# In a hybrid attention layer, the weighted sums of one pair of heads are put in front of the scores of the next

## The chip, the cores and the metric

The kernel runs on one core of a Trainium2 chip. The metric is the device time in microseconds (us) of one execution. The core has five engines with their own instruction queues: TensorE (PE, matrix products; its weight loads are shown as PEld), VectorE (DVE), ScalarE (ACT), GpSimd (POOL), and SyncE (SP), which here issues most of the DMAs. An engine works through its own queue in order and waits for the others by semaphores.

## What is computed

One decoder layer on 512 positions of width 1024, in float32, with two attention branches of 8 heads of 64 each, side by side:

```
h = rms_norm(x);  qa,ka,va,za, qb,kb,vb,zb, gl_a,gl_b = split(h @ w_in)
a: softmax(rms_norm(qa) @ rms_norm(ka).T * scale + T5 bias, causal) @ va
b: w[t,s] = sigmoid(z) * prod_{s<j<t} (1 - sigmoid(z[t,j])),  z = qb @ kb.T * scale;   w @ vb
y = sigmoid(gl_a + b_a) * ((oa * silu(za)) @ w_up_a) + sigmoid(gl_b + b_b) * ((ob * silu(zb)) @ w_up_b)
x + y @ w_out
```

Branch a is a block-sparse attention, but with 512 positions every block of the past is chosen, so the kernel computes plain causal attention.

## The kernel before

The projections come first: q, k and v of branch a and v of branch b for all positions. Everything that remains of the input projection (gates `za`, `zb`, `gl`, and q, k of branch b) is cut into chunks of 128 output columns (`chunk_ct`). One chunk is 24 matmuls of 512 columns: eight slices of the width, each in three products (L179 to L181) of a value that is split into a high and a low part (`hi`, `lo`; `wh` is written by ACT at L138, the remainder `wl` by DVE at L140, from a weight tile `wr` that SP loads at L129).

The main loop (L601) runs over eight pairs of heads, pairs 0 to 3 of branch a, 4 to 7 of branch b. In each pair:

- `scores` computes the products of q and k of both heads. The heads lie in the upper and the lower 64 partitions, and their matmuls alternate: 24 in all (L418), of 512, 384, 256 and 128 columns, each in three products of split values.
- `softmax` (ACT and DVE) or `stick` (two sigmoids on ACT, a scan and a product on DVE) makes the weights `p` of a head, `turn` transposes them on DVE in blocks (L461), `put` stores them to DRAM (SP, L468), and `get` brings them back fully transposed as `pt` (issued by ACT, L475).
- `fill` puts chunks of projections between these steps, by the list FILLS.
- `finish` of the pair before calls `weighted`: eight matmuls (L487) with `pt` of both heads, alternating, into the two halves of one bank `po`, head 0 into partitions 0 to 63 and head 1 into 64 to 127. These run in plain float32. DVE multiplies the result with the gate (`oa` or `ob`, L491), and `split_o` splits it into `oh` (ACT, L522) and `ol` (DVE, L523), which the `up` products use later.

The order in which instructions stand on an engine is set by a scheduler that takes the source's order as a priority and moves an instruction back when it reckons that its operands come late. Accumulation banks come from two pools, "pj" with two banks for chunks and `po`, "s" with six for scores.

Of the kernel before, what the change touches and what calls it, by code (L numbers as in the profile page):

```python
# [57 lines left out]
def hybrid_layer(ctx: ExitStack, tc: tile.TileContext, x, xT, w, rel, out):  # L58
# [15 lines left out]
    def bank(tag, name):  # L74
        return pp.tile([P, S], F32, tag=tag, bufs=BANKS[tag], name=name)
# [23 lines left out]
    def sum_w(names, done):  # L99

        with tc.issue_after(G.tensor_copy(turn_of, done[:1, :1].bitcast(F32)).ins):  # L101
            for n in range(2):
                for name in names:
                    if n == 0:
                        sums[name] = vp.tile([P, H // 2, 2, P], F32, tag="v", name=name).rearrange("p a b d -> p (a b d)")
                    blk = TERMS[name[:2]][n]
                    src = sums[blk + name[2]] if blk[0] == "T" else w[WO + BLOCKS.index(blk + name[2])]
                    nc.gpsimd.dma_start(sums[name], src, **({"accum_op": ALU.add} if n else {}))
# [165 lines left out]
    def load_bias(h):  # L274
        bt = oms[2 + h % 2][:, :S]
        nc.sync.dma_start(bt, bass.AP(tensor=e_dr.tensor, offset=e_dr.offset + h * TW, ap=[[1, P], [1, S]]))
        return bt
# [129 lines left out]
    def scores(br, p, q, k, res):  # L407

        (qh, ql), (kh, kl) = q[p], k[p]
        for grp in ((3,), (2,), (1, 0)):  # L410
            ps = [bank("s", f"s{br}{2 * p + b}{grp[0]}") for b in range(2)]
            c = 0
            for i in grp:
                n = (i + 1) * P
                for m, (x, y) in enumerate(((qh, kl), (ql, kh), (qh, kh))):
                    for b in range(2):
                        o = slice(b * HD, (b + 1) * HD)
                        T.matmul(ps[b][:, c:c + n], x[o, i * P:(i + 1) * P], y[o, :n], start=m == 0, stop=m == 2)  # L418
                for b in range(2):
                    res[2 * p + b][i] = ps[b][:, c:c + n]  # L420
                c += n
# [32 lines left out]
    def turn(br, h, rows):  # L454
        turned = tp.tile([P, 4, BLK[-1], 32], F32, tag="turned", bufs=2, name=f"turned{br}{h}")
        for i in (3, 2, 1, 0):
            for j in range(0, i + 1, 2):
                n = min(2, i + 1 - j)
                step = (BLK[j + 1] - 1 - BLK[j]) if n == 2 else 1
                at = BLK[j] + i - j  # L460
                V.transpose(turned[:, :, at:at + (n - 1) * step + 1:step, :].rearrange("p q j r -> p j q r"),  # L461
                            rows[i][:, j * P:(j + n) * P].rearrange("p (j q c) -> p j q c", j=n, q=4))
        return turned

    def put(br, h, turned):
        dr = dp.tile([P, 4 * PQ], F32, tag="pd", bufs=4, name=f"pd{br}{h}")
        for a in range(4):
            nc.sync.dma_start(bass.AP(tensor=dr.tensor, offset=dr.offset + a * PQ,  # L468
                                      ap=[[4 * PQ, 32], [32 * 4 * PQ, 4], [1, PQ]]),
                              turned[a * 32:(a + 1) * 32].rearrange("c q k r -> c q (k r)"))  # L470
        return dr

    def get(br, h, dr):
        pt = tp.tile([P, 4 * PQ], F32, tag="pt", bufs=4, name=f"pt{br}{h}")
        nc.scalar.dma_start(pt, dr)  # L475
        return pt
# [3 lines left out]
    def weighted(tag, br, p, vv, pts):  # L480

        po = bank(tag, f"po{br}{p}")
        for j in range(NT):
            for b in range(2):
                o, c = slice(b * HD, (b + 1) * HD), (2 * p + b) * HD
                src = pts[b].rearrange("p (a n) -> p a n", a=4)[:, :, BLK[j] * 32:BLK[j + 1] * 32]
                T.matmul(po[o, :].rearrange("p (a n) -> p a n", a=4)[:, :, j * 32:], vv[j][:, c:c + HD], src,  # L487
                         start=j == 0, stop=j == NT - 1, skip_group_check=True)
        ocol[br, p] = u = slot(f"o{br}{p}")
        dst, z = (by_block((mirror if br == "a" else blocks)(x)) for x in (u, zr[br, p]))  # L490
        V.tensor_tensor(dst, po.rearrange("p (a i r) -> p a i r", a=4, i=4).rearrange("p a i r -> p i a r"), z,  # L491
                        op=ALU.mult)
# [25 lines left out]
    def split_o(br, p):  # L518
        u = ocol[br, p]
        oH[br, p] = slot(f"oh{br}{p}", F32R)  # L520
        oL[br, p] = slot(f"ol{br}{p}", F32R)
        A.activation(oH[br, p], u, AF.Copy)  # L522
        V.tensor_tensor(oL[br, p], u, oH[br, p].bitcast(F32), op=ALU.subtract)  # L523
# [59 lines left out]
    def fill(tag="pj"):  # L583

        home[0] = tag
        for kind, i in fills.pop(0):
            make[kind](i)
# [4 lines left out]
    def head(m, b):  # L592
        return PAIRS[m][0], 2 * PAIRS[m][1] + b

    def finish(m, tag="s"):

        br, p = PAIRS[m]
        weighted(tag, br, p, v_of[br], [done.pop((m, b)) for b in range(2)])
        split_o(br, p)

    for m, (br, p) in enumerate(PAIRS):  # L601
        q, k = (qa, ka) if br == "a" else (qb, kb)
        sc, rw = {h: [None] * NT for h in (2 * p, 2 * p + 1)}, {h: [None] * NT for h in (2 * p, 2 * p + 1)}
        scores(br, p, q, k, sc)
        if m > 1:
            finish(m - 1, "pj")
        for b in range(2):
            h = 2 * p + b
            bias = load_bias(h) if br == "a" else None
            (softmax if br == "a" else stick)(h, sc[h], rw[h], bias, (3, 2, 1, 0))  # L610
            done[m, b] = put(br, h, turn(br, h, rw[h]))
            fill()
            if not b:
                done[m, 0] = get(*head(m, 0), done[m, 0])
        for b in range(2):
            if m == 1 and not b:
                finish(0)
            if not b:
                done[m, 1] = get(*head(m, 1), done[m, 1])
            if (m, b) in SUMS:  # L620
                sum_w(SUMS[m, b], done[m, b])
            fill("pj" if b or not fills[1] and m < len(PAIRS) - 1 else "s")
# [87 lines left out]
    for c in range(2):  # L710
        hi, lo = load_w()
        for t, ps, a, b in parts:
            for kk in range(2):
                k = 2 * c + kk
# [76 lines left out]
```

## Time and profile before

| | |
|---|---|
| time, median of three runs | 391.37 us (391.12 to 391.51) |
| the profiled execution's own time | 391.4 us |
| its span, from the first to the last instruction | 389.6 us |
| PE busy | 385.0 us, 99% |
| DVE, ACT, POOL busy | 68%, 50%, 13% |
| mean granted TensorE clock | 0.999 of full speed |

A share of busy time is an average over the whole program. What an edit costs is read from the place where it stands: from the list of who waited for whom, and from the timeline of the engine that others wait for.

### The profile page before, as it was taken

Reading aid. Unit: us, or ns where it says so; the run is one execution under the profiler, and the core shown is the slowest. Engines: PE = TensorE matmul, PEld = TensorE weight load, DVE = VectorE, ACT = ScalarE, POOL = GpSimd, SP = SyncE. Lnnn points to the kernel's source line nnn. Section 1 sums busy time; section 2 is a strip of 40 time slices with the busy share of each in tenths; the row PEclk is TensorE's granted clock in tenths of the full one; section 3 lists DMA queues with packets and bytes.
Section 4 is the critical chain, followed back from the end, with each engine's and each line's share of the span. In section 5 each row is a group of like instructions: output and inputs, shape, how many; then the busy total and the mean of one; then the engine's idle time right before and its main releaser. Section 6 shows DMA issues by size and latency. Waiting matters only on the chain.

```text
span 389.6 us, 5321 instructions
## 1 busy us (share of the span) xinstructions
PE 385.0 (99%) x1853; PEld 308.8 (79%) x1853; DVE 266.8 (68%) x535; ACT 194.6 (50%) x341; POOL 51.9 (13%) x100
## 2 busy tenths in 40 slices
PE   8999999999999999999999999999999999999996
PEld 5888888888887878878788878878878878888885
DVE  4824995854879477295596398489459534999962
ACT  5684522945778466264552472363254232359540
POOL 1018966000000000000000100100000000232110
PEclk9999999999999999999999999999999999999999
DMA  7977259982496946827526776776772842798935
GB/s 266 330 269 241 112 157 290 307 273 73 133 259 226 295 178 151 306 74 240 175 68 192 257 202 182 246 205 170 263 215 67 271 148 89 217 245 301 196 76 175
DMA packets 36091, 79.29 MB, mean 203 GB/s; under 512 B 3929, under 2 KB 16729, under 8 KB 36065
## 3 DMA queue, kind: packets, MB, share of 16 engines
q1 hardware_dynamic: 29584, 56.68, 45.0%
q0 software_dynamic: 2880, 9.44, 10.6%
q10 hardware_dynamic: 3600, 12.85, 9.9%
q8 instruction: 14, 0.23, 0.2%
q14 instruction: 13, 0.10, 0.1%
HBM read 62.15 MB, written 14.70 MB: 197 GB/s over the span
## 4 chain that ended last, share of the span: by engine, by line
PE 99%; DVE 0%; issue 0%
PE gl L179 8%; PE gl L181 7%; PE gl L180 7%; PE poa L487 2%; PE pob L487 2%; PE sb L418 2%; PE sa L418 2%; PE za L179 2%; PE kb L179 2%; PE zb L179 2%; PE za L180 2%; PE kb L181 2%; PE zb L181 2%; PE zb L180 2%; PE yb L181 2%; PE yb L180 2%
## 5 line engine op out<-in xcount | busy, mean ns | idle before, releaser
L140 DVE TENSOR_TENSOR wl<-wr,wh 128x1024 fp32r<-128x1024 f32 (+1 forms) x64 | 75.8, 1185 | 62.1 <-ACT wh L138 57.0
L138 ACT ACTIVATE wh<-wr 128x1024 fp32r<-128x1024 f32 (+1 forms) x64 | 65.8, 1028 | 41.4 <-DMA wr<-in_w 15.8
L179 PE MATMUL gl<-xl,wh 128*128 128x512 f32 x128 | 50.5, 395 | 0.0
L181 PE MATMUL gl<-xh,wh 128*128 128x512 f32 x128 | 49.9, 390 | 0.0
L180 PE MATMUL gl<-xh,wl 128*128 128x512 f32 x128 | 49.8, 389 | 0.0
L513 ACT ACTIVATE gl<-gl,x 128x512 f32<-128x512 f32 x16 | 11.0, 690 | 41.7 <-PE gl L181 41.6
L179 PEld LDWEIGHTS gl<-xl,wh 128*128 128x128 f32 x128 | 24.0, 188 | 5.8 <-issue 1.0
L101 POOL COPY turn_of<-ptb 1x1 f32<-1x1 f32 x3 | 1.3, 433 | 202.0 <-DMA ptb<-pdb 202.0
L181 PEld LDWEIGHTS gl<-xh,wh 128*128 128x128 f32 x128 | 24.0, 188 | 5.1
L180 PEld LDWEIGHTS gl<-xh,wl 128*128 128x128 f32 x128 | 24.0, 188 | 4.8
L446 DVE TENSOR_TENSOR_SCAN sx<-om,begin 128x512 f32<-128x512 f32 (+3 forms) x32 | 24.9, 805 | 0.2 <-ACT om L442 0.2
L430 ACT ACTIVATE pa<-pa,m 128x512 f32<-128x512 f32 (+3 forms) x32 | 17.8, 557 | 10.9 <-DVE m L428 9.0
L428 DVE CUSTOM_DVE_ANT_0 pa<-sa,om 128x512 f32<-128x512 f32 (+3 forms) x32 | 14.8, 477 | 10.9 <-PE sa L418 10.9
L461 DVE STREAM_TRANSPOSE turneda<-pa 128x256 f32<-128x256 f32 (+1 forms) x48 | 16.4, 376 | 0.1
L442 ACT ACTIVATE om<-sb 128x512 f32<-128x512 f32 (+3 forms) x32 | 14.6, 462 | 3.2 <-DVE sx L446 2.9
L461 DVE STREAM_TRANSPOSE turnedb<-pb 128x256 f32<-128x256 f32 (+1 forms) x48 | 15.9, 370 | 0.0
L444 ACT ACTIVATE pb<-sb 128x512 f32<-128x512 f32 (+3 forms) x32 | 14.7, 465 | 0.0
L448 DVE TENSOR_TENSOR pb<-pb,sx 128x512 f32<-128x512 f32 (+3 forms) x32 | 14.2, 471 | 0.0
L179 PE MATMUL za<-xl,wh 128*128 128x512 f32 x32 | 12.7, 396 | 0.0
L179 PE MATMUL kb<-xl,wh 128*128 128x512 f32 x32 | 12.6, 393 | 0.0
L179 PE MATMUL zb<-xl,wh 128*128 128x512 f32 x32 | 12.6, 393 | 0.0
L181 PE MATMUL zb<-xh,wh 128*128 128x512 f32 x32 | 12.5, 390 | 0.0
(305 smaller groups left out, 957.9 us busy)
## 6 DMA issues: line engine op xcount, KB each, us to landing
wr<-in_w SPq DMA_DIRECT2D x60, 512.0 KB, 5.4
pda<-turneda SPq DMA_DIRECT2D x32, 160.0 KB, 2.6
pta<-pda ACTq DMA_DIRECT2D x8, 640.0 KB, 6.0
pdb<-turnedb SPq DMA_DIRECT2D x32, 160.0 KB, 2.7
ptb<-pdb ACTq DMA_DIRECT2D x8, 640.0 KB, 4.5
xn<-in_x SPq DMA_DIRECT2D x8, 256.0 KB, 6.6
xs<-in_xT SPq DMA_DIRECT2D x8, 256.0 KB, 6.2
om<-e_dr SPq DMA_DIRECT2D x8, 256.0 KB, 6.5
```

Source lines behind the costliest of these rows:

```text
L138: A.activation(hi[:, a:b], raw[:, a:b], AF.Copy)
L140: low[c] = V.tensor_tensor(lo[:, a:b], raw[:, a:b], hi[:, a:b].bitcast(F32), op=ALU.subtract).ins
L179: T.matmul(ps, aH, bL, start=start, stop=False, skip_group_check=on)
L180: T.matmul(ps, aL, bH, start=False, stop=False, skip_group_check=on)
L181: T.matmul(ps, aH, bH, start=False, stop=stop, skip_group_check=on)
L418: T.matmul(ps[b][:, c:c + n], x[o, i * P:(i + 1) * P], y[o, :n], start=m == 0, stop=m == 2)
L428: V.tensor_tensor_reduce(p, sc[i], bias[:, S - n:], scale=1.0, scalar=3e38, op0=ALU.add, op1=ALU.min, accum_out=m[:, 0:1])
L430: A.activation(p, p, AF.Exp, bias=m[:, 0:1], scale=-1.0, accum_out=m[:, 1:2])
L444: A.activation(p, z, AF.Sigmoid)
L446: V.tensor_tensor_scan(sx[:, n - 1::-1] if n == S else sx[:, :n][:, ::-1], om[:, e - n:][:, ::-1], begin[:, S - n:][:, ::-1], 0.0, op0=ALU ...
L461: V.transpose(turned[:, :, at:at + (n - 1) * step + 1:step, :].rearrange("p q j r -> p j q r"), rows[i][:, j * P:(j + n) * P].rearrange("p ...
L487: T.matmul(po[o, :].rearrange("p (a n) -> p a n", a=4)[:, :, j * 32:], vv[j][:, c:c + HD], src, start=j == 0, stop=j == NT - 1, skip_group ...
```

## The change

The call of `finish` for the pair before stands in front of `scores` and not behind it, from pair 2 on.

```
     for m, (br, p) in enumerate(PAIRS):
         q, k = (qa, ka) if br == "a" else (qb, kb)
         sc, rw = ...
-        scores(br, p, q, k, sc)
         if m > 1:
             finish(m - 1, "pj")
+        scores(br, p, q, k, sc)
         for b in range(2):
...
```

The built programs show what the scheduler makes of it. First PE at the boundary of pair 2. In the program before, the last scores of pair 2 (`sa`), then the eight weighted matmuls of pair 1 (`poa`, from the transposed tiles `pta` of its two heads), then the next chunk (`gl`); the number behind a name counts tiles:

```order
L418 MATMUL sa_1446<-ka2h,qa2l 128x128
L418 MATMUL sa_1445<-ka2h,qa2h 128x128
L418 MATMUL sa_1446<-ka2h,qa2h 128x128
L487 MATMUL poa_1459<-pta_1274,vas_803 64x512
L487 MATMUL poa_1459<-pta_1361,vas_803 64x512
L487 MATMUL poa_1459<-pta_1274,vas_803 64x4x96
L487 MATMUL poa_1459<-pta_1361,vas_803 64x4x96
L487 MATMUL poa_1459<-pta_1274,vas_806 64x4x64
L487 MATMUL poa_1459<-pta_1361,vas_806 64x4x64
L487 MATMUL poa_1459<-pta_1274,vas_806 64x4x32
L487 MATMUL poa_1459<-pta_1361,vas_806 64x4x32
L179 MATMUL gl_1517<-xl_112,wh_1365 128x512
```

The eight stand together, head 0 (`pta_1274`) and head 1 (`pta_1361`) in turn. Now PE at the same boundary in the changed program, from the last matmul of the chunk on:

```order
L181 MATMUL gl_1402<-xh_261,wh_1315 128x512
L487 MATMUL poa_1429<-pta_1274,vas_803 64x512
L418 MATMUL sa_1444<-ka2l,qa2h 128x512
L418 MATMUL sa_1445<-ka2l,qa2h 128x512
L418 MATMUL sa_1444<-ka2h,qa2l 128x512
L418 MATMUL sa_1445<-ka2h,qa2l 128x512
L418 MATMUL sa_1444<-ka2h,qa2h 128x512
L418 MATMUL sa_1445<-ka2h,qa2h 128x512
L418 MATMUL sa_1452<-ka2l,qa2h 128x384
L418 MATMUL sa_1453<-ka2l,qa2h 128x384
L418 MATMUL sa_1452<-ka2h,qa2l 128x384
L487 MATMUL poa_1429<-pta_1361,vas_803 64x512
```

One weighted matmul, that of head 0, moved in front; nine scores follow, then the other seven weighted matmuls in a row (the first of them is the last row here), then the remaining 15 scores. At pair 3 it is the same with ten scores between, at pair 4 with eleven.

Second, PE at the boundary of pair 5 in the changed program (`kb` is the chunk in front, `pob` the weighted sums of pair 4, `sb` the scores of pair 5):

```order
L181 MATMUL kb_2214<-xh_261,wh_2137 128x512
L487 MATMUL pob_2243<-ptb_2061,vbs_957 64x512
L487 MATMUL pob_2243<-ptb_2133,vbs_957 64x512
L487 MATMUL pob_2243<-ptb_2061,vbs_957 64x4x96
L487 MATMUL pob_2243<-ptb_2133,vbs_957 64x4x96
L487 MATMUL pob_2243<-ptb_2061,vbs_960 64x4x64
L487 MATMUL pob_2243<-ptb_2133,vbs_960 64x4x64
L487 MATMUL pob_2243<-ptb_2061,vbs_960 64x4x32
L487 MATMUL pob_2243<-ptb_2133,vbs_960 64x4x32
L418 MATMUL sb_2258<-kb1l,qb1h 128x512
```

Here, and at pairs 6 and 7, the block of eight moved as a whole in front of the 24 scores.

Third, DVE at the start of pair 4, where `sx` is a scan of the stick-breaking weights, `pb` the weights, `qb1l` a split of q, `wl` the remainder of a weight tile, `oa` the gated result of the weighted sums. In the program before:

```order
L310 SCALAR_TENSOR_TENSOR qb1l<-qb_1916,qb1h 128x512
L446 SCALAR_TENSOR_TENSOR sx_1993<-om_334,begin 128x512
L446 SCALAR_TENSOR_TENSOR sx_1999<-om_333,begin 128x384
L448 TENSOR_TENSOR pb_1991<-pb_1991,sx_1993 128x512
L448 TENSOR_TENSOR pb_1997<-pb_1997,sx_1999 128x384
L461 STREAM_TRANSPOSE turnedb_2014<-pb_1991 128x2x4x32
```

The scans begin right behind `qb1l`; `oa` stands five rows further down, `wl_2029` behind all of the head. In the changed program DVE has, at the same place:

```order
L310 SCALAR_TENSOR_TENSOR qb1l<-qb_1916,qb1h 128x512
L140 TENSOR_TENSOR wl_2029<-wr_2026,wh_2028 128x1024
L491 TENSOR_TENSOR oa_1954<-poa_1945,za_1271 128x4x128
L446 SCALAR_TENSOR_TENSOR sx_1993<-om_334,begin 128x512
L446 SCALAR_TENSOR_TENSOR sx_1999<-om_333,begin 128x384
L523 TENSOR_TENSOR ola_1957<-oa_1954,oha_1956 128x512
L448 TENSOR_TENSOR pb_1991<-pb_1991,sx_1993 128x512
```

`wl_2029` and `oa` moved in front of the first scan. ACT has four table loads more in the changed program (an exponential now stands behind a sigmoid of a chunk in pairs 2 and 3, and pair 4 begins with a load), and on SP one load of a weight tile moved in front of the eight stores of pair 4's tiles.

## Rows read from the trace of the kernel before

**Rows 1.** The page: span, busy time and share of each engine, and the engines' shares of the chain that ended last.

```profile
span 389.6 us, 5321 instructions
PE 385.0 (99%) x1853; PEld 308.8 (79%) x1853; DVE 266.8 (68%) x535; ACT 194.6 (50%) x341; POOL 51.9 (13%) x100
...
PE 99%; DVE 0%; issue 0%
```

**Rows 2.** The list of waits for PE alone, whole: who waited for whom, us in total, times, longest.

```profile
PE pwarm L172 <- DVE warm L86: 1.0, 1, 1.0
```

**Rows 3.** PE's timeline at the boundary of pair 2: start, length (to the end of the last one's pipeline, so that rows overlap), line, tiles, count. The last row before the scores is the end of a chunk, the last of all the start of the next.

```profile
137.38 0.39 PE L180 MATMUL gl<-xh,wl 128*128 128x512 f32 x1
137.60 0.39 PE L181 MATMUL gl<-xh,wh 128*128 128x512 f32 x1
137.92 0.50 PE L418 MATMUL sa<-ka2l,qa2h 64*128 64x512 f32 x2
138.26 0.40 PE L418 MATMUL sa<-ka2h,qa2l 64*128 64x512 f32 x2
138.49 0.40 PE L418 MATMUL sa<-ka2h,qa2h 64*128 64x512 f32 x2
...
138.91 0.34 PE L418 MATMUL sa<-ka2h,qa2l 64*128 64x384 f32 x2
139.08 0.34 PE L418 MATMUL sa<-ka2h,qa2h 64*128 64x384 f32 x2
...
139.79 0.27 PE L418 MATMUL sa<-ka2h,qa2h 64*128 64x128 f32 x2
139.99 2.38 PE L487 MATMUL poa<-pta,vas 128*64 128x512 f32 x16
142.29 0.50 PE L179 MATMUL gl<-xl,wh 128*128 128x512 f32 x1
```

**Rows 4.** The chain that ended last, in order of time: start, time on the chain, work. At 92.83 scores stand in front of a chunk, at 124.59 weighted sums stand between two chunks, at the others scores stand in front of weighted sums.

```profile
92.83 2.07 PE sa L418 x24
...
124.59 2.31 PE poa L487 x16
...
164.37 2.07 PE sa L418 x24
166.43 2.31 PE poa L487 x16
...
222.55 2.07 PE sb L418 x24
...
254.37 2.07 PE sb L418 x24
```

**Rows 5.** PE's weight loads (timeline) in the first block of weighted sums, which stands alone between two chunks: start, length, count. The first row has the loads of the first two passes.

```profile
124.51 0.20 PEld L487 LDWEIGHTS poa<-pta,vas 128*64 128x64 f32 x4 [0.35 <-DVE m L431]
125.00 0.14 PEld L487 LDWEIGHTS poa<-pta,vas 128*64 128x64 f32 x2 [0.29 <-issue]
125.43 0.14 PEld L487 LDWEIGHTS poa<-pta,vas 128*64 128x64 f32 x2 [0.29 <-issue]
125.75 0.14 PEld L487 LDWEIGHTS poa<-pta,vas 128*64 128x64 f32 x2 [0.18 <-issue]
```

**Rows 6.** The transposed tiles of head 1, of pairs 1 to 5 in order: their issue on ACT's queue (timeline), and from the list of DMA issues in the same stretches the size and the time from issue to landing.

```profile
132.81 0.33 ACTq L475 DMA_DIRECT2D pta<-pda  x1
159.19 0.33 ACTq L475 DMA_DIRECT2D pta<-pda  x1
185.56 0.33 ACTq L475 DMA_DIRECT2D pta<-pda  x1
212.88 0.33 ACTq L475 DMA_DIRECT2D ptb<-pdb  x1
244.65 0.33 ACTq L475 DMA_DIRECT2D ptb<-pdb  x1
...
pta<-pda ACTq DMA_DIRECT2D x1, 640.0 KB, 6.0
pta<-pda ACTq DMA_DIRECT2D x1, 640.0 KB, 5.8
pta<-pda ACTq DMA_DIRECT2D x1, 640.0 KB, 4.0
ptb<-pdb ACTq DMA_DIRECT2D x1, 640.0 KB, 8.3
ptb<-pdb ACTq DMA_DIRECT2D x1, 640.0 KB, 6.1
```

**Rows 7.** DVE's timeline in pair 4: the first row is in front of its scans, the last the end of the transposes of head 1; between them DVE has no idle time.

```profile
191.41 0.69 DVE L310 SCALAR_TENSOR_TENSOR qb1l<-qb,qb1h 128x512 fp32r<-128x512 f32 x1 [3.26 <-ACT qb1h L309]
192.30 2.07 DVE L446 TENSOR_TENSOR_SCAN sx<-om,begin 128x512 f32<-128x512 f32 x2 [0.20 <-ACT om L442]
...
199.70 1.19 DVE L140 TENSOR_TENSOR wl<-wr,wh 128x1024 fp32r<-128x1024 f32 x1
...
205.87 1.80 DVE L461 STREAM_TRANSPOSE turnedb<-pb 128x256 f32<-128x256 f32 x6
```

**Rows 8.** ACT's timeline in pair 2, behind the last exponential of head 1: the load of the sigmoid's table and the first sigmoid of a chunk.

```profile
149.39 1.28 ACT L513 ACT_TABLE_LOAD   x1
...
150.69 0.69 ACT L513 ACTIVATE gl<-gl,x 128x512 f32<-128x512 f32 x1
```

More of the change, by code (lines that the diff above doesn't have):

```diff
@@ L603, in hybrid_layer @@
         sc, rw = {h: [None] * NT for h in (2 * p, 2 * p + 1)}, {h: [None] * NT for h in (2 * p, 2 * p + 1)}
-        scores(br, p, q, k, sc)
         if m > 1:
             finish(m - 1, "pj")
+        scores(br, p, q, k, sc)
         for b in range(2):
```

## The prediction

> **What bounds the kernel now.** I read the page first. TensorE (PE) is busy 385.0 of 389.6 us, and the chain that ended last is PE for 99% of the span [rows 1]. Then its waits: the whole list holds one entry, 1.0 us for the warm-up tile at the start [rows 2]. So PE never waits inside the program; the time is the sum of what PE streams, and an edit counts if it adds to or takes from that stream, or makes PE wait. DVE (68%) and ACT (50%) matter only where they are late for PE.
>
> Last the PE timeline at a pair's boundary [rows 3]. Scores start in twos: two heads (64 rows of the array each) run side by side, 0.23 us for two 512-column matmuls (138.26 to 138.49), 0.17 for two of 384 (138.91 to 139.08). The weighted sums, too: their weights are loaded in twos, and the twos follow each other after 0.49, 0.43, 0.32 us [rows 5], 512, 512, 384 columns. Sixteen records answer to eight matmuls: each is two passes, and one two is the same pass of both heads. A block of scores takes 2.07 us and a block of weighted sums 2.31, whatever neighbour it has: scores in front of a projection or of weighted sums, weighted sums behind a projection or behind scores [rows 4].
>
> **What the built order makes of it.** The source moves one call, the scheduler more. At pairs 5, 6 and 7 the two blocks change places whole. At pairs 2, 3 and 4 only the first weighted matmul (head 0, 512 columns) goes in front; 9, 10 and 11 scores follow, then the other seven weighted, then the other scores.
>
> **The cost, step by step.**
> 1. Pairs 5 to 7: the same two blocks in the other order. By [rows 4] a block's length doesn't depend on what surrounds it, except that weighted sums in front of scores stand nowhere in this trace. Every change of kind that does stand there costs about 0.2 us: into scores 0.32 in place of 0.22 for the start and 0.34 in place of 0.23 for the next [rows 3]; into weighted sums 0.20 in place of about 0.1 [rows 3] and 0.49 in place of 0.43 [rows 5]. Three changes before, three after: 0. Bounds: 0 to 0.4 for the new kind, so -0.6 to +0.6 over three pairs.
> 2. Pairs 2 to 4, the lone matmul. Its two passes take 0.43 us each [rows 5], 0.86, and nothing runs beside it. The remaining seven still have head 1's four in line, 512 + 384 + 256 + 128 columns in two passes, as long as the block was; head 0's three run beside them. So 0.86 is added per pair, 2.6 in all. Bounds: 0, if the twos were two halves of one matmul and the heads ran one after the other, and 0.91 (124.51 to 125.43, entry included). I take 0.86, since the scores show two heads side by side in the same form.
> 3. Pairs 2 to 4, changes of kind: projection, weighted, scores, weighted, scores, projection is five in place of three. Two more at 0.2 us, three times: 1.2 (bounds 0 and 2.4).
> 4. Pairs 2 and 4 cut the scores at an odd place (9 and 11), which leaves one 384-column matmul alone: 0.17 each [rows 3], 0.35 in all.
>
> PE's stream grows by 2.6 + 1.2 + 0.35 = 4.1 us.
>
> 5. What the boundaries now wait for. The second weighted matmul needs head 1's transposed tile (issued by ACT at L475). Landing [rows 6] against the time at which PE reaches it: pair 2: 132.81 + 6.0 = 138.8; PE gets there at 137.92 + 1.0 (lone matmul) + 1.16 (nine scores) + 0.1 = 140.2. Pair 3: 159.19 + 5.8 = 165.0, and 1.4 later with PE (its issue stands behind a sigmoid that waits for PE), 166.4; reached at about 164.4 + 1.4 + 2.4 = 168.2. Pair 4: 185.56 + 4.0 + 2.7 = 192.3; reached past 195. At pairs 5 to 7 nothing covers it, the tile must be there when the block starts. Pair 6: 244.65 + 6.1 = 250.8 for a block at 254.4 [rows 4, 6]; pair 5's chain starts about 1 us later than before, margin 2.5. Pair 5 is the narrow place: 212.88 + 8.3 = 221.2 for a block at 222.5. DVE works through pair 4's heads without a break from 192.30 to 207.67 [rows 7]. In the new order it does the 1.2 us remainder of a weight, then waits for the weighted sums (`oa`), which now end some 4.8 us after the boundary starts (lone matmul 1.0, scores 1.3, rest 2.3, changes), before its first scan: it idles about 2.1 us that it didn't, so head 1's tile is 2.4 us later, 223.6, while PE itself is 1.4 us later, 223.9. Margin 0.3: no wait taken, 0 to 2 us kept for the range.
> 6. Covered edits. Four more table loads on ACT, 1.28 us each [rows 8], because an exp now stands behind a projection's sigmoid: in pair 2 that sigmoid ran at 150.69 [rows 8] and I have it end at about 153, after two loads; the third projection of the pair needs its bank at 142.3 + 1.4 + 2 x 5.5 = 154.7 (24 matmuls of 0.23). Free by 1.8 us. On SP one weight load passes the eight stores of pair 4's tiles; it waits for the DVE remainder that moved to the front, so it doesn't hold them. `oa` and its split come earlier or at the same time, and are used from the first `ya` on.
>
> **Sum.** The profiled execution took 391.4 us (span 389.6), beside a median of 391.37; 391.4 + 4.1 = 395.5 us.
>
> **Rivals.**
> - *Head 1's tile is late* at pair 5, or at pair 3: for it speak the 8.3 us landing and the margin of 0.3; against it that the other four landings took 4.0 to 6.1, and that a weight load now leaves before these transfers. It adds 0.5 to 2.5: 396 to 398. On the page "TensorE: Matmul & The Clock Gate" (Part 3, The mechanism) the Trainium skill has matmuls start and end in strict order, so a late tile would stop the scores behind it as well; no wait of this kind stands in this trace.
> - *The rest runs out of step*: after the lone one the stream is head 1, head 0, head 1, each of another size. If heads run side by side only when they come as in the old block, seven matmuls take 2.1 us for head 1's and 1.3 for head 0's (768 columns in two passes at 0.43 for 512): 1.3 more per pair, 399.4. For it: the trace shows no other pairing than equal sizes. Against: scores show neighbours of different heads starting within 0.01 us with nothing else in common than form.
> - *ACT and DVE become the bound in pairs 2 and 3*: the two table loads hold a sigmoid, that a bank, that PE. It decides when the sigmoid ends more than 1.8 us later than I have it; then 1 to 2 us per pair, 397 to 399.
> - *The lone matmul is no loss* (the low bound of step 2): 391.4 + 1.2 + 0.35 = 393.0.
> - *Not slower*: the lone matmul uses half of the array's columns, and the scores behind it start beside it. Then 0.86 and the changes around it are hidden, and what stays is below 0.8 us: 391.4 to 392.2, and below 391 if weighted-to-scores costs nothing. It decides when the scores start less than about 0.3 us after the lone matmul's start. Against it: every change of kind in the trace has a later start, never an earlier one. The Trainium skill says under "TensorEngine Tiling (Array Packing)" (Key Properties) that changing the tiling mode drains the engine, which excludes this case and gives no price; the trace agrees as far as it goes, with 0.32 in place of 0.22 at such a place [rows 3].
>
> That the change does nothing can't be: the stream has another order. No rival makes PE's stream shorter by a part that a row shows.
>
> **Chances.** Forecast (395.0 to 396) 0.55; late tile 0.17; out of step 0.10; ACT and DVE 0.05; lone matmul free 0.07; not slower 0.06. Range: without the last two cases and most of the out-of-step one, 0.8 remain between 393.4 (just above the free lone matmul, with room for the price of the changes) and 398.5. By 0.2% (0.8 us, about what a measurement of this kernel can tell from no change): slower 0.93, same 0.05, faster 0.02.
>
> **What would show it.** PE's timeline at pairs 2 to 4: a lone weighted matmul in two passes of 0.43 and the scores about 1.0 us behind its start; the boundary 5.6 to 5.8 us in place of 4.37 (137.92 to 142.29). At pairs 5 to 7: 4.4, blocks of 2.31 and 2.07. PE's list of waits still short: an entry for `ptb` at pair 5 would be the late tile, one for ACT at a projection the table loads. Wrong I'd be if the boundaries stayed below 5 us (pairing or overlap misread) or passed 6 (out of step, or a wait).

## The result, and the profile after

The changed kernel takes 395.27 us (median of four runs, 395.0 to 395.96), beside 391.44 us (391.12 to 391.75) for the kernel before in the same comparison: a ratio of 1.0102, with a 95% interval of 1.009 to 1.0114. The forecast was 395.5 us. The profiled execution took 395.37 us, with a span of 393.6 us in place of 389.6 [rows 1].

The page of the changed kernel: span, busy time of each engine, and the engines' shares of the chain that ended last.

```profile
span 393.6 us, 5343 instructions
PE 388.0 (99%) x1853; PEld 309.8 (79%) x1853; DVE 268.5 (68%) x535; ACT 199.9 (51%) x345; POOL 52.9 (13%) x100
...
PE 91%; DMA 4%; DVE 2%; ACT 1%; issue 0%; SPq 0%; ACTq 0%
```

PE has as many matmuls as before (1853) and is busy 3.0 us longer; 1.0 us more of the span is idle. The chain is no longer PE alone: from 142.29 to 168.01 it goes through DVE, ACT, the stores and the load of a transposed tile (and in the opening through a weight's load and ACT). The list of PE's waits names the place (who waits for whom, us in total, times, longest):

```profile
PE pwarm L172 <- DVE warm L86: 1.0, 1, 1.0
PE qa L206 <- ACT wh L138: 0.6, 1, 0.6
PE poa L487 <- DMA pta<-pda: 0.4, 1, 0.4
```

The second entry lies in the opening, ahead of everything that the change moves, and varies from run to run (0.6 here, 0.2 to 0.4 in some of the kernels below, absent in others). The third comes with the change: PE waits for head 1's transposed tile.

PE's timeline at the boundary of pair 2, which answers to [rows 3] (start, length to the end of the last one's pipeline, tiles, count):

```profile
137.65 1.07 PE L487 MATMUL poa<-pta,vas 128*64 128x512 f32 x2
138.65 0.50 PE L418 MATMUL sa<-ka2l,qa2h 64*128 64x512 f32 x2
...
139.89 2.37 PE L487 MATMUL poa<-pta,vas 128*64 128x512 f32 x14
142.19 0.44 PE L418 MATMUL sa<-ka2h,qa2l 64*128 64x384 f32 x1
...
143.37 0.50 PE L179 MATMUL gl<-xl,wh 128*128 128x512 f32 x1
```

The boundary, from its first matmul to the next chunk, takes 143.37 - 137.65 = 5.72 us, in place of 142.29 - 137.92 = 4.37 [rows 3]. The lone weighted matmul (two records, its two passes) holds PE for 1.00 us, the other seven for 2.30 us, as long as all eight did. Pair 3 has the same form, with the wait in it (in brackets: idle time ahead of the row, and its cause):

```profile
165.34 1.07 PE L487 MATMUL poa<-pta,vas 128*64 128x512 f32 x2
166.34 0.50 PE L418 MATMUL sa<-ka3l,qa3h 64*128 64x512 f32 x2
...
168.06 2.37 PE L487 MATMUL poa<-pta,vas 128*64 128x512 f32 x14 [0.41 <-DMA pta<-pda]
170.35 0.44 PE L418 MATMUL sa<-ka3h,qa3h 64*128 64x384 f32 x2
...
171.36 0.50 PE L179 MATMUL gl<-xl,wh 128*128 128x512 f32 x1
```

That is 6.02 us. Pair 4 takes 5.74 us (193.35 to 199.09), without a wait. At pair 5, where the block moved whole:

```profile
226.54 2.37 PE L487 MATMUL pob<-ptb,vbs 128*64 128x512 f32 x16
228.84 0.50 PE L418 MATMUL sb<-kb1l,qb1h 64*128 64x512 f32 x2
...
230.91 0.50 PE L179 MATMUL zb<-xl,wh 128*128 128x512 f32 x1
```

4.37 us, to the hundredth what it was. So the time went to three places: 1.35 us at pair 2, 1.65 at pair 3, 1.37 at pair 4, together 4.4 us. Ahead of pair 2 this execution is 0.27 us earlier than that of before (137.65 against 137.92). 4.4 less 0.27 is 4.1 us; the spans differ by 4.0.

### The profile page after: what moved, and what is told of

It is laid out like the page before. It is cut to its first block, busy times and chain, and to the rows that moved or that the text cites. A ratio compares the mean times of both kernels' runs of the same rounds, so it can differ in the third digit from the quotient of the medians.

```text
span 393.6 us, 5343 instructions
## 1 busy us (share of the span) xinstructions
PE 388.0 (99%) x1853; PEld 309.8 (79%) x1853; DVE 268.5 (68%) x535; ACT 199.9 (51%) x345; POOL 52.9 (13%) x100
## 4 chain that ended last, share of the span: by engine, by line
PE 91%; DMA 4%; DVE 2%; ACT 1%; issue 0%; SPq 0%; ACTq 0%
PE gl L179 6%; PE gl L181 6%; PE gl L180 6%; PE poa L487 3%; PE pob L487 2%; PE sb L418 2%; PE za L179 2%; PE kb L179 2%; PE zb L179 2%; PE za L180 2%; PE zb L180 2%; PE kb L181 2%; PE yb L181 2%; PE yb L180 2%; PE ya L179 2%; PE qb L179 2%
## 5 line engine op out<-in xcount | busy, mean ns | idle before, releaser
L461 DVE STREAM_TRANSPOSE turnedb<-pb 128x256 f32<-128x256 f32 (+1 forms) x48 | 15.0, 367 | 0.1
L487 PE MATMUL poa<-pta,vas 128*64 128x256 f32 (+3 forms) x64 | 12.7, 441 | 0.4 <-DMA pta<-pda 0.4
```

## The experiments

Three questions were put: does the cost lie at pairs 2 to 4 alone, how much of it is the lone matmul and how much the changes of kind, and why a block in front of the scores is cut there at all. Two attempts to save changes of kind follow. A change of kind is a place in PE's stream where it goes from one of projections, scores and weighted sums to another.

**Pairs 2 to 4 alone, pairs 5 to 7 alone.**

```
-        if m > 1:
+        if 1 < m < 5:                  # the other kernel: m > 4
             finish(m - 1, "pj")
         scores(br, p, q, k, sc)
+        if m > 4:                      # the other kernel: 1 < m < 5
+            finish(m - 1, "pj")
```

> Theory (what a split costs): the weighted sums stand in front of the scores at pairs 2 to 4 alone, where the scheduler tears them apart; pairs 5 to 7 are as before. All of the loss is there: 1.3 us more of PE's stream per boundary (blocks of 5.7 us in place of 4.37) and the 0.4 us wait for head 1's tile at pair 3: 395.3 us, as the changed kernel. Rival (the place itself costs, the same at each of the six boundaries): half of the loss, 393.4.

> Theory: the weighted sums stand in front at pairs 5 to 7 alone, whole. The boundaries there take 4.37 us as before and head 1's tiles have landed: 391.4 us, no change (within 0.3). Rival (the place costs): 393.4.

With the block in front at pairs 2 to 4 alone: 395.12 us, ratio 1.0102 (1.0085 to 1.0119), the whole of the change's cost. The expected wait is not in this trace's list: head 1's tile landed at 167.70, the seven of pair 3 started at 167.74, and the boundary took 5.70 us (165.36 to 171.06) in place of the 6.02 above. Up to there PE's order is the same in both kernels, so the length of this wait is not fixed. At pairs 5 to 7 alone: 391.17 us, ratio 0.9999 (0.9989 to 1.0008): exchanging two whole blocks costs nothing. Three changes of kind stand against three, and the kind that is new, from weighted sums into scores, has the price of the others.

**Twelve changes of kind more.** The place of before, but at pairs 4 to 7 the two blocks are cut into five pieces; no matmul is without its partner. The edit in outline:

```
-        scores(br, p, q, k, sc)
-        if m > 1: finish(m - 1, "pj")
+        scores, group 3            (6 matmuls)
+        weighted, j = 0            (2)
+        scores, group 2            (6)
+        weighted, j = 1, 2, 3      (6)
+        scores, groups 1 and 0     (12)
```

> The place of before, but from pair 4 on scores and weighted sums are cut into each other with heads always in twos: 6 scores, 2 weighted, 6 scores, 6 weighted, 12 scores. Three more changes of kind per boundary at four boundaries, no lone matmul, no wait. Theory: 0.2 us per change, 12 changes, 2.4 us: 393.8, boundaries of 4.97 us. Rivals: a change costs nothing once both operands are there: 391.4; or the changes make up the whole of the split's cost (1.3 us for two changes, 0.65 each): 399.

It took 393.46 us, ratio 1.0055 (1.004 to 1.007): 2.26 us for twelve changes, 0.19 each. PE's timeline of this kernel at pair 4:

```profile
190.95 0.50 PE L418 MATMUL sb<-kb0l,qb0h 64*128 64x512 f32 x2
...
191.84 1.08 PE L494 MATMUL poa<-pta,vas 128*64 128x512 f32 x4
192.85 0.44 PE L418 MATMUL sb<-kb0l,qb0h 64*128 64x384 f32 x2
...
195.86 0.50 PE L179 MATMUL kb<-xl,wh 128*128 128x512 f32 x1
```

4.91 us in place of 4.37. The second row also prices the lone matmul: here both heads' first weighted matmuls, four records, hold PE for 192.85 - 191.84 = 1.01 us. In the changed kernel head 0's alone held it for 1.00 us. One matmul without a partner costs as much as two with one.

**The heads one after the other.** Head 0's four weighted matmuls, then head 1's four, in all eight blocks.

```
-        for j in range(NT):
-            for b in range(2):
+        for b in range(2):
+            for j in range(NT):
```

> The program of before, but the weighted sums take the four matmuls of head 0 first and then the four of head 1, in all eight blocks. Theory (a matmul of one head has nothing beside it unless the next in line is the other head's): the two heads overlap only at the seam, each takes 2.1 us, a block 4.1 us in place of 2.31: 8 x 1.8 = 14 us more, 405 to 407. Rival (each half of the array has its own line and starts the other head's matmuls as they come, far ahead): 391.4, and then the lone matmul of the changed kernel is lone only because its partner's tile was awaited. Second rival (twos are two passes of one matmul): 391.4 too, with twos of the same head.

403.47 us, ratio 1.0312 (1.0292 to 1.0333), 1.54 us per block; the expectation had 1.8. The first block takes 3.86 us (123.93 to 127.79) in place of 2.30. Its weight loads come singly, where those of [rows 5] come in twos:

```profile
124.42 0.14 PEld L487 LDWEIGHTS poa<-pta,vas 128*64 128x64 f32 x1 [0.29 <-issue]
124.84 0.14 PEld L487 LDWEIGHTS poa<-pta,vas 128*64 128x64 f32 x1 [0.29 <-issue]
125.17 0.14 PEld L487 LDWEIGHTS poa<-pta,vas 128*64 128x64 f32 x1 [0.18 <-issue]
```

The steps are those of [rows 5], 0.42 and 0.33 us, with one matmul's pass in each and not two. So the two heads do run side by side, if they alternate in the stream.

**The block in front, kept whole.** At pairs 2 to 7 PE's later work may be issued only behind the last weighted matmul, so that the scheduler can't cut the block (`finish` here also returns that matmul).

```
+        end = finish(m - 1, "pj") if m > 1 else None
+        behind = ExitStack()
         if m > 1:
-            finish(m - 1, "pj")
+            behind.enter_context(tc.issue_after(end))
         scores(br, p, q, k, sc)
         ...                            # the rest of the pair
+        behind.close()
```

> The same place as in the changed kernel, but the eight weighted matmuls are kept together at every pair, in front of all scores. Theory: no lone matmul and no more changes of kind, so every boundary streams in 4.37 us, and what is lost at pairs 2 to 4 is only the wait for head 1's tile at the start of the block: about 1.0 us at pair 2 (landed 138.6, block at 137.65), 1 to 2 at pair 3, 0 to 1 at pair 4; 393.4 to 395.4, with PE waits on the transposed tiles in the list. Rival (the place costs by itself, the split nothing): 395 plus these waits, 397 to 399, with boundaries above 5 us beyond the waits.

It took 399.27 us, ratio 1.0195 (1.0176 to 1.0215), 4 us above the highest figure of the theory, which left out what the cut was covering. PE's waits and its timeline at the boundaries of pairs 2, 3 and 4:

```profile
PE poa L487 <- DMA pta<-pda: 3.7, 2, 3.0
```

```profile
137.44 3.36 PE L487 MATMUL poa<-pta,vas 128*64 128x512 f32 x16
140.73 0.50 PE L418 MATMUL sa<-ka2l,qa2h 64*128 64x512 f32 x2
...
164.75 1.07 PE L487 MATMUL poa<-pta,vas 128*64 128x512 f32 x2
168.82 3.83 PE L487 MATMUL poa<-pta,vas 128*64 128x512 f32 x14 [3.00 <-DMA pta<-pda]
172.58 0.50 PE L418 MATMUL sa<-ka3l,qa3h 64*128 64x512 f32 x2
...
196.61 1.07 PE L487 MATMUL poa<-pta,vas 128*64 128x512 f32 x2
198.41 2.37 PE L487 MATMUL poa<-pta,vas 128*64 128x512 f32 x14 [0.73 <-DMA pta<-pda]
200.71 0.50 PE L418 MATMUL sb<-kb0l,qb0h 64*128 64x512 f32 x2
```

At each of the three, head 0's first matmul runs alone again, because head 1's tile isn't there: the trace has it landing at 138.39, 168.78 and 198.37, and head 1's first matmul starts 0.04 us later each time. The blocks take 3.29, 7.83 and 4.10 us in place of 2.30. At pair 3 there is a third cost: after the idle time PE runs at half its clock (columns: window, its length, busy time and count of PE, PEld, DVE, ACT and POOL, granted clock, DMA):

```profile
168.80:170.40 1.60, 1.58 (x5) 0.96 (x7) 0.00 (x0) 0.00 (x0) 0.00 (x0) 0.50 0.76 276
```

0.50 is 1.2 GHz in place of 2.4, and the remaining seven take 3.76 us in place of 2.30. At pairs 5 to 7, where the tile is there, boundaries take 4.36 us. The rival's time came out, but not its cause: what these three take above 4.37 us is the lone matmul, the wait and the clock, and pairs 5 to 7, at the same place in the order, take no more than before. So the cut can't simply be taken away: it puts scores into a wait that would otherwise be open.

**The block in front, with its tile there.** At pairs 3, 4 and 5 the sums of the pair before the last stand in front of the scores; those of pair 4 stand between two chunks of pair 5, and pairs 6 and 7 are as in the changed kernel.

```
-        if m > 1:
-            finish(m - 1, "pj")
+        if m > 2:
+            finish(m - 2 if m < 6 else m - 1, "pj")
         scores(br, p, q, k, sc)
         ...
-            if m == 1 and not b:
-                finish(0)
+            if m in (1, 5) and not b:
+                finish(m - 1)
```

> In front of the scores of pairs 3, 4 and 5 stand the weighted sums of the pair before the last (pairs 1, 2, 3), whose tiles landed long before; those of pair 4 stand between two chunks of pair 5; pairs 6 and 7 as in the changed kernel. The scheduler keeps every block of eight whole. Theory (a block in front of the scores costs nothing by its place; the changed kernel pays for head 1's tile, which lands after the boundary, so that the block is cut behind its first matmul): against the kernel before, one change of kind less at pair 2, two more at pair 5, 0.2 us net: 391.2 + 0.2 = 391.4 us (391.0 to 391.9), boundaries at pairs 3, 4 and 5 of 4.4 us and no wait of PE for a tile. Rival (weighted sums in front of scores cost something at pairs 2 to 4 whatever the tile does, 1.2 us each as in the changed kernel): 394.5 or more, boundaries above 5 us.

391.21 us, ratio 0.9999 (0.999 to 1.0008). PE has no wait for a tile, every block is whole, and the boundaries take 4.35 to 4.37 us. At pair 3:

```profile
161.71 2.37 PE L487 MATMUL poa<-pta,vas 128*64 128x512 f32 x16
...
166.07 0.50 PE L179 MATMUL gl<-xl,wh 128*128 128x512 f32 x1
```

This settles the cause: weighted sums in front of scores are free at pairs 3 and 4, too (pair 2 has none in front here), when the tile has landed before PE arrives. The 0.2 us that a net one more change should have cost can't be told from zero here (the last block starts 0.2 us earlier than before, and this execution is 0.26 us ahead by the first block already).

**The wait at pair 3.** The changed kernel, but in pairs 2 and 3 the first chunk is written behind head 1's softmax, so that no sigmoid falls between its exponentials. PE's order is the same.

```
             done[m, b] = put(br, h, turn(br, h, rw[h]))
-            fill()
+            for _ in range((0, 2)[b] if m in (2, 3) else 1):
+                fill()
```

> The changed kernel, with the first chunk of pairs 2 and 3 put behind head 1's softmax in the source, so that no sigmoid stands between the exponentials and ACT has as few table loads as before; PE's order is the same. Theory: head 1's tile of pair 2 was late because its last exponential stood behind two table loads and a chunk's sigmoid (DVE waited 1.8 us for it); without them the 0.41 us wait at pair 3 is gone, 394.9, and nothing else changes. Rival (the tile is late by its transfer alone): the wait stays, 395.3.

394.85 us, ratio 1.0095 (1.008 to 1.011). The intervals of this and of the changed kernel overlap, so the times alone don't show the wait's share; the trace does. PE's list has no wait for `pta`, and at pair 3 the seven now start without one:

```profile
165.29 1.07 PE L487 MATMUL poa<-pta,vas 128*64 128x512 f32 x2
...
167.53 2.37 PE L487 MATMUL poa<-pta,vas 128*64 128x512 f32 x14
...
170.84 0.50 PE L179 MATMUL gl<-xl,wh 128*128 128x512 f32 x1
```

The boundary takes 5.55 us in place of 6.02, and the other two 5.72 and 5.74 as before. What made the tile late stands in the changed kernel's timelines of pair 2, first ACT's:

```profile
150.45 1.28 ACT L513 ACT_TABLE_LOAD   x1
151.74 0.69 ACT L513 ACTIVATE gl<-gl,x 128x512 f32<-128x512 f32 x1
152.45 1.28 ACT L430 ACT_TABLE_LOAD   x1
153.75 0.40 ACT L430 ACTIVATE pa<-pa,m 128x128 f32<-128x128 f32 x1
```

Then SP's, with the last four stores of head 1's tile: in the changed kernel, in the kernel before, and in this run, one row each:

```profile
155.13 1.87 SPq L468 DMA_DIRECT2D pda<-turneda  x4
...
151.34 1.76 SPq L468 DMA_DIRECT2D pda<-turneda  x4
...
152.89 2.95 SPq L468 DMA_DIRECT2D pda<-turneda  x4
```

And from the changed kernel's chain that ended last, the last of these stores and the transposed load (start, time on the chain):

```profile
156.44 5.32 DMA pda<-turneda
...
161.85 6.16 DMA pta<-pda
```

A sigmoid between two table loads delays head 1's last exponential by 3.3 us; the transposes and the stores follow it. The stores left 3.79 us later than in the kernel before, and with no sigmoid and no table load between the exponentials 2.24 us of that are gone. In the changed kernel the last store landed at 161.76, the transposed load left at 161.85, and the tile was there at 168.01, in this run at 165.82.

**Two attempts to save changes of kind.** First the kernel before, with pair 0's block moved directly in front of pair 1's, behind the scores of pair 2:

```
-            if m == 1 and not b:
-                finish(0)
...
+        if m == 2:
+            finish(0)
         if m > 1:
             finish(m - 1, "pj")
```

> The program of before, with the weighted sums of pair 0 taken out from between two chunks and put directly behind the scores of pair 2, in front of those of pair 1. Two changes of kind fewer, nothing lone. Theory: 0.2 us each, 0.4 less: 391.0, at the edge of what can be measured; the block of sixteen takes 4.4 to 4.45 us in place of 2 x 2.30. Rival (a wait for a tile or a bank that the move brings): 391.4 or more.

392.33 us, ratio 1.003 (1.002 to 1.004). The two changes of kind fall away, but PE now reaches head 1's tile of pair 1 too early (it landed at 140.03), and head 0's first matmul is alone once more: the sixteen take 5.49 us, where two single blocks take 4.61.

```profile
136.89 5.56 PE L487 MATMUL poa<-pta,vas 128*64 128x512 f32 x32
142.38 0.50 PE L179 MATMUL gl<-xl,wh 128*128 128x512 f32 x1
```

This trace is of the shortest of nine executions (391.49 us); the other eight took 392.0 to 392.92, and what they spent in addition no trace shows.

Second, two pairs' blocks together behind the scores of pairs 3, 5 and 7:

```
-        if m > 1:
+        if m in (3, 5, 7):
+            finish(m - 2, "pj")
             finish(m - 1, "pj")
```

> The kernel before, but the weighted sums of pairs 1 and 2 stand together behind the scores of pair 3, those of 3 and 4 behind the scores of pair 5, those of 5 and 6 behind the scores of pair 7. Three places where PE goes from scores to weighted sums fall away, at 0.19 us each (as the run with twelve more changes of kind gave): 391.2 - 0.6 = 390.6 us (390.3 to 391.0), and the second block starts 2.3 us later than a single one, so that its tile has more room than before. Rival (two blocks take both banks of the chunks' pool, and the next chunk waits until DVE has multiplied the first one with its gate, 0.5 to 1.5 us at each of three places): 391.5 to 395, with waits of PE for DVE's oa or ob.

399.47 us, ratio 1.021 (1.0196 to 1.0224): the rival, and dearer than it said. The two blocks take both banks of "pj", and the next chunk waits for DVE, which is in the middle of head 0's scans. PE's waits, then PE's timeline at pair 5, then DVE's at the same place:

```profile
PE zb L179 <- DVE oa L491: 2.5, 1, 2.5
PE gl L179 <- DVE ob L491: 2.5, 1, 2.5
```

```profile
229.41 0.77 PE L179 MATMUL zb<-xl,wh 128*128 128x512 f32 x1 [2.51 <-DVE oa L491]
```

```profile
228.61 0.65 DVE L491 TENSOR_TENSOR oa<-poa,za 128x512 f32<-128x512 f32 x1
```

The two waits are 5.0 us. Behind each PE again runs at the lower clock for some 3 us (the granted clock has a mean of 0.58 from 229.4 to 233.0 and of 0.56 from 296.8 to 300.4), and 0.74 us go at pair 3, where the second block is ahead of its tile. None of the kernels beat the one before.

## Why the prediction was right

**Step 1** (pairs 5 to 7, 0 with bounds of 0.6): right, by the run with these alone, 391.17 against 391.20. In the new order the blocks take 2.30 and 2.06 us, within 0.01 of the old [rows 4].

**Step 2** (the lone matmul, 0.86): right. Lone, it holds PE for 1.00 us, a change of kind included; less 0.19 that is 0.81. The seven that remain take 2.30, as the eight did. Both halves of the reasoning were tried by themselves: heads that don't alternate cost 1.54 us a block, and a pair takes as long as a single one (1.01 and 1.00).

**Step 3** (a change of kind at 0.2, six more): right in size, 0.19 by the run with twelve. On the page "TensorEngine Tiling (Array Packing)", Key Properties, the Trainium skill has a change of tiling mode drain the engine. The trace agrees so far as a change costs time, 0.19 us as a mean; that it is a drain which takes it, no run shows.

**Step 4** (an odd cut of the scores, 0.17): right. Without waits the boundaries of pairs 2, 3 and 4 take 5.72, 5.55 and 5.74; the two odd ones are 0.17 and 0.19 above the even one.

So the sum without waits is 1.35 + 1.18 + 1.37 = 3.9 us, where the prediction had 4.1.

**Step 5** (all tiles land in time) is the step that failed, at pair 3, though it changed the time little. The prediction moved the landing later only by the 1.4 us of the boundary, because the load's issue had stood behind a sigmoid that waits for PE, and left a margin of 1.8 us. In fact the tile landed at 168.01 and not at 166.4, and PE was there at 167.65 and not at 168.2. By then the sigmoid was no longer the last thing that the load waited for; the stores were, 3.79 us later than before, 2.24 of it on account of the table loads and the sigmoid between them. The prediction had counted these loads in step 6 and had followed only the sigmoid behind them to the bank, not the exponential behind them to the stores. The cost is 0.47 us (6.02 - 5.55) in this execution, 0.15 in that with pairs 2 to 4 alone (5.70). It made up for the 0.2 by which the sum without waits was too high, and the two together, 4.4, less 0.27 of the opening, gave a span 4.0 us longer. That the forecast came within 0.3 us of the time is luck in part: a sum too high by 0.2, a wait that it held at nothing, and a shorter opening offset each other. At pair 4, too, the tile came later than reckoned (194.57 against 192.3), but still ahead of the seven at 195.78.

At pair 5, the margin called narrow (0.3), the danger didn't come. DVE did idle as foreseen, in front of `oa`, 1.93 us where the prediction had 2.1:

```profile
198.18 0.69 DVE L491 TENSOR_TENSOR oa<-poa,za 128x512 f32<-128x512 f32 x1 [1.93 <-PE poa L487]
```

Against before, head 1's load left 4.57 us later (217.45), and PE reached the boundary 4.06 us later (226.54 against 222.48): a loss of 0.5 us, where the prediction had 1.0. What made the margin wide is the load itself, in the list of DMA issues:

```profile
ptb<-pdb ACTq DMA_DIRECT2D x1, 640.0 KB, 5.4
```

5.4 us in place of the 8.3 of [rows 6], so that it landed at 222.89, 3.65 us ahead of the block. Why it was 8.3 before was not tried.

**Step 6** (four more table loads, covered): right for PE's banks, no wait of a chunk for ACT behind the opening; not harmless, as step 5 has it.

**The rivals.** The late tile came in a mild form, 0.47 us at pair 3, within the forecast's range. The rest out of step (1.3 us per pair) is refuted by the seven at 2.30. ACT or DVE as the bound and the free lone matmul don't occur. Not slower: the scores start 1.00 us behind the lone matmul, not within 0.3. The Trainium skill's strict order ("TensorE: Matmul & The Clock Gate", Part 3, The mechanism), cited for what a late tile would do, agrees with pair 3, where the scores behind the fourteen records waited with them until 170.35. Among the seven themselves it doesn't hold, by the last section's second point.

What the prediction did not ask is why the block is cut at pairs 2 to 4 and not at 5 to 7. The landings agree with the scheduler's choice: in the changed kernel head 1's tile lands 1.0, 2.7 and 1.2 us after PE reaches pairs 2, 3 and 4 (138.65, 168.01 and 194.57), and 3.65 us before it reaches pair 5. The lone matmul and the two changes of kind are the price of bridging that gap; left open, it costs twice as much (399.27 against 395.27), and without the gap nothing (391.21).

## What to carry to other kernels

Before work is moved forward in a stream that never waits, compare the landing of each of its operands with the new time of arrival, and follow the chain of that operand through every engine on which the change puts something new. If one operand is late, a scheduler may split the block, and the split has a price of its own: count the matmuls that lose their partner, and the changes between kinds of matmul. Where the operand is in time, a block's place is free.

## What the runs showed of the hardware

- Two float32 matmuls of 64 columns of weights each run side by side in the two halves of the array if they alternate in the stream: 1.01 us for two, 1.00 for one alone, 3.86 us for eight in line against 2.30 alternating.
- In the seven after the lone one, partners have unequal sizes (512 columns beside 384, and so on), and still take 2.30 us. At pair 2 the two heads don't keep one order: the second pass of head 0's 384 columns starts at 140.27 and that of head 1's 512 at 140.37, and head 0's 256 columns start at 140.59, ahead of head 1's 384 at 140.80, though by the source's order head 1 stands first each time.
- A change between kinds of matmul (128 x 128, 64 rows, 64 columns) costs 0.19 us, as a mean over the twelve of one run.
- In the kernel with the blocks kept whole PE resumed after 3.0 us of waiting at a granted clock of 0.50 (seven matmuls in 3.76 us); after a wait of 0.73 us at pair 4 the granted clock was 1.00 (2.30 us).
